# Second feed-forward product of a hybrid encoder layer: four accumulators a row pair, last chunk in two groups of rows, first operands made during the first product

## The chip, the cores and the metric

One core of one Trainium2 chip. The metric is the device time of one execution in microseconds (us); three executions are shown for the kernel before, and one further execution was recorded by the hardware profiler. All durations below are of that profiled execution.

## The reference, cut to what matters

The input is 2048 rows of 1024 numbers, in float32. One layer mixes them (a gated MLP and a gated linear attention), projects, and adds; this part takes about the first 780 us and its arithmetic is not touched. Then comes the feed-forward part:

```
f = rmsnorm(h, pre_ff_g) @ w_ff1          # 2048 x 1024 times 1024 x 4096
f = square(relu(f)) @ w_ff2               # 2048 x 4096 times 4096 x 1024
h = h + rmsnorm(f, post_ff_g)             # the output
```

The change concerns the second of these products, its normalisation, and the passage from the first product to the second.

## The kernel before, in words

**Numbers in two parts.** Every matmul operand is a pair: `hi`, rounded to a shorter format by the scalar engine (ACT), and `lo`, the rest, a subtraction on the vector engine (DVE). One product of two such operands is three matmuls (`mm3`, lines 142 to 145): high by low, high by high, low by high, each 128x128 by 128x512.

**Seven products in place of eight.** Both feed-forward products go by a Strassen-Winograd scheme (`WINO`, lines 40 and 41): of two 2x2 blocked operands seven block products p1 to p7 are made, from sums s1 to s4 of the left blocks and t1 to t4 of the right ones. p1, p6, p7 and p4 are added up in one PSUM bank (chain A), p5 and p3 in a second one (C), p2 in a third (B). Read after each step, the banks hold what the output blocks need: block 11 is p1 plus p2, block 12 is A after p6 plus C after p3, block 22 is A after p7 plus C after p5, block 21 is A after p4.

**The first product** (lines 696 to 927) runs in 224 ticks of 12 matmuls: 2 halves of the rows (p) by 16 pieces of the 4096 columns (q) by 7 products. Its results go to memory (`f_d`, written by `keep_f`, lines 859 to 866). The sums and splits of `w_ff2` are also made during it and stored as 1 MB tiles (`t_d`, lines 823 to 829). DVE, ACT, GpSimd (POOL) and SyncE (SP) follow an order written out by hand (`plan`, `do`, `tick`); line 928 closes that order.

**The second product** (lines 934 to 1133) has 16 chunks, 0 to 15: 2 halves of the rows (p) by 8 pieces of the 4096 terms (c). A chunk has 28 slots: 7 products (order `SECOND`, line 46) by 4 row blocks r; a slot is 6 matmuls (2 pieces kk by `mm3`). For each product the right operand is a 1 MB tile `tt`, read by `read_t` (lines 981 to 985) two products ahead into one of three buffers. The left operands come from `f_d`: `read_f` (lines 943 to 948, 512 KB each, four a chunk, into the four `xr` tiles), `sum_f`, `high_f` (ACT) and `low_f` (DVE). Before the loop all operands of chunk 0 are made (lines 1017 to 1030) in an order that the framework chooses; from line 1032 on the order is again that of the program. There `PREP` (lines 988 to 995) says in which slot of the chunk before each of the 22 steps of a chunk comes (two casts and two sums first, the last step in slot 23), `SHIFT` by how many slots later, `READ` that the next chunk's tiles are read in the slots 18 to 21 of this count.

**Out of PSUM** (`evac`, lines 1065 to 1091): after each slot its bank is added to an accumulator. There are seven a row pair, one for each product and r, 28 tiles (line 1069). In the first piece (c = 0) ACT copies, afterwards DVE adds; in the last piece DVE also folds three of the seven into others (lines 1076 to 1079), and the four that remain are the blocks 11, 12, 21, 22.

**The end of a row.** `square_sum` (ACT) sums the squares of each finished half row; `root` (two DVE operations of one column and a power on POOL, line 153) makes the factor; `scale` (DVE, line 1059) multiplies; `give` (line 1062) adds the row of h that `read_h` brought, and sends the half row out (256 KB). For the first half of the rows these steps wait in the list `tail` and are worked off from chunk 8 on, one or two a slot, and `give` is on DVE, its transfer on POOL's queue. For the second half they follow two slots after the last product; there `give` is on POOL for the rows of block 21 and 22 and on DVE for the others.

**Where tiles lie.** Pools are stacked from the left and from the right end of SBUF. During the first product the right side holds `wq` (the split pieces of `w_ff1`) and `fr` (20 tiles of the right operand and 3 staging tiles `w2s`), the left one `big`. When they close, `g` takes the place of `big` on the left, and `ga` (accumulators) and then `gt` (the three `tt` buffers) that of `wq` and `fr`. A tile in the new place waits for the last use of what lay there.

## Time and profile before

| | us |
|---|---|
| three executions | 2084.5, 2089.95, 2090.33 (median 2089.95) |
| the profiled execution | 2087.72 |
| its span, first to last instruction | 2085.9 |
| DVE busy | 1424.2 (68%) |
| ACT busy | 995.7 (48%) |
| POOL busy | 253.4 (12%) |
| mean granted TensorE clock | 0.989 of full |
| moved by DMA | 446.85 MB, 214 GB/s on the mean |

The profiled execution is 2.2 us below the median and 1.8 us longer than its span. The first feed-forward product begins shortly before 790 us of the span, the second at about 1426. Busy times are sums over stages with different limits; what a stage is worth is read from the stage's own rows. In the timeline a row gives the start, the time, the engine and line, the operation with output and inputs, and in brackets how long the engine was idle before it and what ended that.

### The profile page before, as it was taken

How to read it: one execution, taken by the hardware profiler on the slowest of the kernel's cores; microseconds unless marked ns; L12 is line 12 of the kernel's file. 1: busy time of each engine (PE TensorE's matmuls, PEld its weight loads, DVE VectorE, ACT ScalarE, POOL GpSimd, SP SyncE). 2: the span in 40 equal slices, each digit the busy share in tenths (PEclk: the TensorE clock that was granted, in tenths of full speed). 3: DMA queues.
4: the chain of work that ended last, by engine and by line, in shares of the span. 5: the costliest groups of instructions: out<-in, count | busy, mean ns of one | idle time of the engine just before them, and what ended most of it. 6: DMA issues, size and time to landing. Idle time of an engine off the chain costs nothing.

```text
span 2085.9 us, 27424 instructions
## 1 busy us (share of the span) xinstructions
PE 2014.2 (97%) x9504; PEld 1656.1 (79%) x9504; DVE 1424.2 (68%) x2483; ACT 995.7 (48%) x1966; POOL 253.4 (12%) x407
## 2 busy tenths in 40 slices
PE   8999999999899998999998999997999999999995
PEld 6889887888788877888887788886888888788884
DVE  4484457357736676656668666765688888889887
ACT  5463465346444565556667666665412215312212
POOL 0020011001101200013321333320000001100003
PEclk9999999999999999999999999999999999999998
DMA  7444244425842546858879888776666767876754
GB/s 214 124 117 128 81 142 143 152 72 165 266 162 87 176 167 204 268 181 271 281 254 307 282 277 284 270 254 246 249 255 234 262 242 261 344 274 231 268 196 181
DMA packets 164715, 446.85 MB, mean 214 GB/s; under 512 B 23376, under 2 KB 48480, under 8 KB 150240
## 3 DMA queue, kind: packets, MB, share of 16 engines
q1 hardware_dynamic: 139040, 359.09, 50.9%
q0 software_dynamic: 25536, 86.00, 11.4%
q8 instruction: 75, 1.23, 0.2%
q14 instruction: 64, 0.52, 0.1%
HBM read 319.19 MB, written 125.83 MB: 213 GB/s over the span
## 4 chain that ended last, share of the span: by engine, by line
PE 76%; DMA 9%; DVE 5%; issue 4%; ACT 3%; POOL 2%; SPq 0%; POOLq 0%; DVEq 0%; ACTq 0%
PE po_A L143 5%; PE po_A L144 5%; PE po_A L145 5%; PE pf_A L143 5%; PE pf_A L144 4%; PE pf_A L145 4%; PE pp_o L143 3%; PE po_C L143 3%; PE pp_o L145 2%; PE po_C L144 2%; PE po_C L145 2%; PE pp_o L144 2%; PE pf_C L145 2%; PE pf_C L144 2%; PE pf_C L143 2%
## 5 line engine op out<-in xcount | busy, mean ns | idle before, releaser
L493 DVE TENSOR_TENSOR acc_p<-acc_p,po_A 128x512 f32<-128x512 f32 x224 | 154.1, 688 | 34.9 <-PE po_A L145 20.5
L974 ACT CAST sh_s<-r 128x512 fp32r<-128x512 f32 x96 | 56.6, 619 | 187.0 <-PE po_A L145 109.5
L140 DVE TENSOR_TENSOR wl_s<-s,wh_s 128x512 fp32r<-128x512 f32 x96 | 66.2, 690 | 67.3 <-ACT wh_s L691 67.2
L143 PE MATMUL pf_A<-hl_t,wh_s 128*128 128x512 f32 x256 | 101.8, 398 | 9.5 <-ACT uy L894 6.1
L143 PE MATMUL po_A<-tt,sh_s 128*128 128x512 f32 x256 | 101.0, 394 | 6.1 <-ACT acc_p L1070 2.4
L143 PE MATMUL pp_o<-wl_o,abh 128*128 128x512 f32 x256 | 103.4, 404 | 2.2 <-DVE h L450 2.0
L143 PE MATMUL po_C<-tt,sh_s 128*128 128x512 f32 x256 | 101.3, 396 | 3.0 <-DMA tt<-t_d_t 3.0
L144 PE MATMUL pf_A<-hh_t,wh_s 128*128 128x512 f32 x256 | 101.5, 396 | 0.0
L145 PE MATMUL pf_A<-hh_t,wl_s 128*128 128x512 f32 x256 | 101.2, 395 | 0.0
L218 DVE SCALAR_TENSOR_TENSOR wl_o<-ws_o,outg,wh_o 128x512 fp32r<-128x512 f32 x64 | 47.9, 750 | 78.0 <-ACT wh_o L217 78.0
L144 PE MATMUL po_C<-tt,sh_s 128*128 128x512 f32 x256 | 100.8, 394 | 0.0
L974 ACT CAST sh_a<-f 128x512 fp32r<-128x512 f32 x94 | 55.8, 619 | 94.2 <-DMA f<-f_d 46.0
L145 PE MATMUL po_C<-tt,sl_s 128*128 128x512 f32 x256 | 100.5, 393 | 0.0
L145 PE MATMUL pp_o<-wh_o,abl 128*128 128x512 f32 x256 | 100.5, 393 | 0.0
L144 PE MATMUL po_A<-tt,sh_s 128*128 128x512 f32 x256 | 100.2, 391 | 0.0
L144 PE MATMUL pp_o<-wh_o,abh 128*128 128x512 f32 x256 | 100.1, 391 | 0.0
L145 PE MATMUL po_A<-tt,sl_s 128*128 128x512 f32 x256 | 99.8, 390 | 0.0
L143 PE MATMUL po_A<-tt,sh_a 128*128 128x512 f32 x248 | 97.4, 393 | 0.0
L144 PE MATMUL po_A<-tt,sh_a 128*128 128x512 f32 x248 | 97.1, 391 | 0.0
L145 PE MATMUL po_A<-tt,sl_a 128*128 128x512 f32 x248 | 96.6, 390 | 0.0
L140 DVE TENSOR_TENSOR wl_a<-w1s,wh_a 128x512 fp32r<-128x512 f32 x96 | 65.9, 687 | 43.4 <-ACT wh_a L691 43.4
L217 ACT ACTIVATE wh_o<-ws_o,outg 128x512 fp32r<-128x512 f32 x64 | 46.3, 723 | 100.6 <-PE pp_o L145 56.2
(298 smaller groups left out, 6043.6 us busy)
## 6 DMA issues: line engine op xcount, KB each, us to landing
tt<-t_d_t SPq DMA_DIRECT2D x64, 1024.0 KB, 4.9
tt<-t_d_b SPq DMA_DIRECT2D x48, 1024.0 KB, 4.8
w1s<-in_w SPq DMA_DIRECT2D x64, 512.0 KB, 4.8
f<-f_d SPq DMA_DIRECT2D x64, 512.0 KB, 7.0
ws_o<-in_w_out SPq DMA_DIRECT2D x64, 256.0 KB, 2.5
w2s<-in_w POOLq DMA_DIRECT2D x32, 512.0 KB, 6.2
t_d_t<-th_t POOLq DMA_DIRECT2D x64, 256.0 KB, 4.8
t_d_t<-tl_t POOLq DMA_DIRECT2D x64, 256.0 KB, 4.6
```

The lines of the kernel that those rows point to most:

```text
L140: v.tensor_tensor(out_lo, src, hi.bitcast(F32), ALU.subtract)
L143: pe.matmul(ps, ahi, blo, start=start, stop=False, **kw)
L144: pe.matmul(ps, ahi, bhi, start=False, stop=False, **kw)
L145: pe.matmul(ps, alo, bhi, start=False, stop=stop, **kw)
L217: a.activation(hi, st, AF.Copy, scale=gain)
L218: v.scalar_tensor_tensor(lo, st, gain, hi.bitcast(F32), ALU.mult, ALU.subtract)
L493: eng.tensor_tensor(out_, x_, y_, ALU.add)
L974: a.copy(hi, src)
```

## The change

- Four accumulators a row pair (11, 12, 22, 21) instead of seven, and 24 tiles for them instead of 28. In the first piece ACT copies the products p1, p6, p5 and p4 into them and DVE adds p7, p3 and p2; after that DVE adds all seven. Nothing is folded in the last piece.
- The last chunk runs in two groups of rows: all seven products for r = 0 and 1, then all seven for r = 2 and 3. Its seven `tt` tiles stay until the second group has used them: three in `gt`, two in the four `xr` tiles (in halves), one in `w2s` tiles (halves), one in four accumulator tiles (quarters).
- `some` works the list `tail` off by one step a slot in the last chunk, and in three of four slots of chunk 7 and each slot of chunk 8. All `give` additions are on DVE. The rows of h for the last chunk are asked for on POOL's queue, all within the slots 2 and 3 of that chunk.
- The left operands of chunk 0 are begun during the last 14 ticks of the first product: four `read_f`, the first `tt` (into `w2s` tiles), the two splits of a11 and the two sums s1. The rest of chunk 0 stands in the slots from -4 on: `SHIFT` is 20 for chunk 0, 16 for chunk 1, then 14, 12, 10, 8, 6, 5, and 4 for chunk 8.
- The pool `wq` moves to the left side; the staging tiles `w2s` become a pool of their own, `br`, that is not closed; `gt` is laid before `ga`. The hand-written order of DVE, ACT, POOL and SP isn't closed between the products. The last `keep_f` and the gain `pfg` go over POOL's queue.

`read_f`, `sum_f`, `high_f` and `low_f` move up unchanged.

```diff
+NACC = 24
...
-    wq = wqp.enter_context(tc.tile_pool(name="wq", bufs=1, side="right", reuse_waits="tile"))
+    wq = wqp.enter_context(tc.tile_pool(name="wq", bufs=1, reuse_waits="tile"))
...
-        nonlocal fr
+        nonlocal fr, br
         if hf == 0 and k == 1:
             mixp.close()
+            br = ctx.enter_context(tc.tile_pool(name="br", bufs=1, side="right", reuse_waits="tile"))
             fr = frp.enter_context(tc.tile_pool(name="fr", bufs=1, side="right", reuse_waits="tile"))
...
-    first = ctx.enter_context(ExitStack())
-    first.enter_context(tc.manual_schedule(engines={ENG.DVE, ENG.Activation, ENG.Pool, ENG.SP}))
+    ctx.enter_context(tc.manual_schedule(engines={ENG.DVE, ENG.Activation, ENG.Pool, ENG.SP}))
...
-        xr = fr.tile([P, D], F32, name=f"xq{i}", tag="w2s", bufs=3)
+        xr = br.tile([P, D], F32, name=f"xq{i}", tag="w2s", bufs=3)
...
-            dma.dma_start(f_d[p][q][:, n, :], us[s][4][n])
+            (dma if s + 1 < NST else pool).dma_start(f_d[p][q][:, n, :], us[s][4][n])
...
+    def read_t(j):
+
+
+        src = t_d[chunks[j // 7][1]][WINO[SECOND[j % 7]][1]]
+        where = {0: "br", 7 * NCH - 7: "xr", 7 * NCH - 6: "xr", 7 * NCH - 5: "br", 7 * NCH - 4: "acc"}.get(j, "tt")
+        if where == "tt":
+            tt = gt.tile([P, 2, 2, 512], F32R, name=f"tt{j}", tag="tt", bufs=3)
+            dma.dma_start(tt.bitcast(F32), src)
+            tts[j] = [[tt[:, kk, m, :] for m in range(2)] for kk in range(2)]
+        elif where == "acc":
+            tts[j] = [[ga.tile([P, 512], F32R, name=f"tt{j}_{kk}_{m}", tag="acc", bufs=NACC) for m in range(2)]
+                      for kk in range(2)]
+            for kk in range(2):
+                for m in range(2):
+                    dma.dma_start(tts[j][kk][m].bitcast(F32), src[:, kk, m, :])
+        else:
+            pool_, tag, bufs = (br, "w2s", 3) if where == "br" else (wp, "xr", 4)
+            two = [pool_.tile([P, 2, 512], F32R, name=f"tt{j}_{kk}", tag=tag, bufs=bufs) for kk in range(2)]
+            for kk in range(2):
+                dma.dma_start(two[kk].bitcast(F32), src[:, kk])
+            tts[j] = [[t[:, m, :] for m in range(2)] for t in two]
+
+
+    end = len(seq)
+    for t, fn, *args in (
+        (end - 14, read_f, 0, 0, 0), (end - 11, read_f, 0, 0, 1), (end - 8, read_t, 0), (end - 7, read_f, 0, 1, 0),
+        (end - 4, read_f, 0, 1, 1), (end - 4, high_f, 0, "a11", 0), (end - 4, low_f, 0, "a11", 0),
+        (end - 3, sum_f, 0, "s1", 0), (end - 2, high_f, 0, "a11", 1), (end - 2, low_f, 0, "a11", 1),
+        (end - 1, sum_f, 0, "s1", 1),
+    ):
+        plan(t, fn, *args)
...
-    first.close()
     frp.close()
     bigp.close()
     wqp.close()
 
 
     g = ctx.enter_context(tc.tile_pool(name="g", bufs=1, reuse_waits="tile"))
+    gt = ctx.enter_context(tc.tile_pool(name="gt", bufs=1, side="right", reuse_waits="tile"))
     ga = ctx.enter_context(tc.tile_pool(name="ga", bufs=1, side="right", reuse_waits="tile"))
-    gt = ctx.enter_context(tc.tile_pool(name="gt", bufs=1, side="right", reuse_waits="tile"))
     pfg = wp.tile([P, D], F32, name="pfg", tag="pg")
-    dma.dma_start(pfg, post_ff_g.partition_broadcast(P))
...
+    pool.dma_start(pfg, post_ff_g.partition_broadcast(P))
...
-        key = WINO[SECOND[j % 7]][1]
-        tts[j] = gt.tile([P, 2, 2, 512], F32R, name=f"tt{j}", tag="tt", bufs=3)
-        dma.dma_start(tts[j].bitcast(F32), t_d[chunks[j // 7][1]][key])
...
-    SHIFT = {NC: 12, NC + 1: 12, NC + 2: 9, NC + 3: 6, NC + 4: 3}
+    SHIFT = {0: 20, 1: 16, 2: 14, 3: 12, 4: 10, 5: 8, 6: 6, 7: 5, NC: 4, NC + 1: 12, NC + 2: 9, NC + 3: 6, NC + 4: 3}
...
-    for m in range(1, NCH):
+    for m in range(NCH):
         o = 28 * (m - 1) + SHIFT.get(m, 0)
         for n, what, name, kk in PREP:
+            if m == 0 and n < 4:
+                continue
             if what == "sum":
                 plan2(o + n, sum_f, m, name, kk)
             else:
 
-                plan2((o + n, 0), high_f, m, name, kk)
+                plan2(o + n - 0.5, high_f, m, name, kk)
                 plan2(o + n, low_f, m, name, kk)
         if m + 1 < NCH:
             for n, half, kk in READ:
                 plan2(o + n, read_f, m + 1, half, kk)
 
-    for n in range(2):
-        for kk in range(2):
-            read_f(0, n, kk)
-    read_t(0)
     read_t(1)
-    for n, what, name, kk in PREP:
-        if what == "sum":
-            sum_f(0, name, kk)
-        else:
-            high_f(0, name, kk)
-            low_f(0, name, kk)
-    for n in range(2):
-        for kk in range(2):
-            read_f(1, n, kk)
-
-    ctx.enter_context(tc.manual_schedule(engines={ENG.DVE, ENG.Activation, ENG.Pool, ENG.SP}))
+    for t in sorted(t for t in todo2 if t < -0.5):
+        for fn, args in todo2.pop(t):
+            fn(*args)
+
     halves, res = {}, {}
...
-                dma.dma_start(res[i][hf], h_d[i][:, hf * 512:(hf + 1) * 512])
+                pool.dma_start(res[i][hf], h_d[i][:, hf * 512:(hf + 1) * 512])
...
-    def give(i, hf, eng, queue):
-        plus(eng, res[i][hf], res[i][hf], halves[i, hf])
+    def give(i, hf, queue):
+        plus(v, res[i][hf], res[i][hf], halves[i, hf])
         queue.dma_start(out[i * P:(i + 1) * P, hf * 512:(hf + 1) * 512], res[i][hf])
+
+
+    INTO = {"p1": 11, "p2": 11, "p6": 12, "p3": 12, "p5": 22, "p7": 22, "p4": 21}
 
     def evac(m, n, r, ps_):
         p, c = chunks[m]
-        x_ = acc.get((p, n, r))
-        if c == 0:
-            acc[p, n, r] = ga.tile([P, 512], F32, name=f"acc{p}_{n}_{r}", tag="acc", bufs=28)
-            a.copy(acc[p, n, r], ps_)
-            return
-        plus(v, x_, x_, ps_)
-        if c < NC - 1:
+        key = p, INTO[n], r
+        if c == 0 and n in ("p1", "p6", "p5", "p4"):
+            acc[key] = ga.tile([P, 512], F32, name=f"acc{p}_{INTO[n]}_{r}", tag="acc", bufs=NACC)
+            a.copy(acc[key], ps_)
+        else:
+            plus(v, acc[key], acc[key], ps_)
+        if c < NC - 1 or n not in ("p7", "p4", "p3", "p2"):
             return
         i, j = p * 2 * NPAIR + r, p * 2 * NPAIR + NPAIR + r
-        if n in ("p1", "p6", "p5"):
-            y_ = acc[p, {"p1": "p2", "p6": "p3", "p5": "p7"}[n], r]
-            plus(v, y_, y_, x_)
-            return
         row_, hf = {"p7": (j, 1), "p4": (j, 0), "p3": (i, 1), "p2": (i, 0)}[n]
-        halves[row_, hf] = x_
+        halves[row_, hf] = acc[key]
         square_sum(row_, hf)
         if hf:
             return
         soon.setdefault(slot_ + 1, []).append((root, row_))
-        if p < NP - 1:
-            tail.extend(((scale, row_, 1), (give, row_, 1, v, pool), (scale, row_, 0), (give, row_, 0, v, pool)))
-        else:
-            eng = pool if row_ == j else v
-            soon.setdefault(slot_ + 2, []).extend((
-                (scale, row_, 1), (give, row_, 1, eng, dma), (scale, row_, 0), (give, row_, 0, eng, dma)))
+        queue = pool if p < NP - 1 else dma
+        for h_ in (1, 0):
+            tail.append((slot_ + 2, scale, row_, h_))
+            tail.append((slot_ + 2, give, row_, h_, queue))
+        if p < NP - 1 and row_ == j:
+
+            tail.append((slot_ + 2, read_h, i - 2) if r > 1 else (0, int))
+        if p < NP - 1 and row_ == i and r < 2:
+            tail.append((slot_ + 2, read_h, i + 2))
+
+    def some(heavy):
+
+        while tail and tail[0][0] <= slot_ and heavy > 0:
+            _, fn, *args = tail.pop(0)
+            fn(*args)
+            heavy -= fn is not read_h
 
     slot_ = 0
     for m, (p, c) in enumerate(chunks):
         banks = {}
-        for n7, n in enumerate(SECOND):
-            name, key, chain = WINO[n]
-            j = 7 * m + n7
-            if j + 2 < 7 * NCH:
-                read_t(j + 2)
-            tt = tts.pop(j)
-            for r in range(NPAIR):
-                begun = (chain, r) in banks
-                if not begun:
-                    banks[chain, r] = bank(f"po{m}_{chain}_{r}", "mm" if chain == "A" else "mx")
-                rs = slice(r * P, (r + 1) * P)
-                for kk in range(2):
-                    hi, lo = left[m, name, kk]
-                    mm3(banks[chain, r], hi[:, rs], lo[:, rs], tt[:, kk, 0, :], tt[:, kk, 1, :],
-                        kk == 0 and not begun, kk == 1, skip_group_check=True)
-                for fn, args in todo2.pop((slot_, 0), ()):
-                    fn(*args)
-                evac(m, n, r, banks[chain, r])
-                for fn, args in todo2.pop(slot_, ()):
-                    fn(*args)
-                for fn, *args in soon.pop(slot_, ()):
-                    fn(*args)
-                for _ in range((2 if slot_ % 4 == 3 else 1) if c < NC - 1 else 0):
-                    if tail:
-                        fn, *args = tail.pop(0)
+        final = m == NCH - 1
+        for grp in ((0, 1), (2, 3)) if final else (range(NPAIR),):
+            for n7, n in enumerate(SECOND):
+                name, key, chain = WINO[n]
+                j = 7 * m + n7
+                if grp[0] == 0 and j + 2 < 7 * NCH:
+                    read_t(j + 2)
+                for r in grp:
+                    begun = (chain, r) in banks
+                    if not begun:
+                        banks[chain, r] = bank(f"po{m}_{chain}_{r}", "mm" if chain == "A" else "mx")
+                    rs = slice(r * P, (r + 1) * P)
+                    for kk in range(2):
+                        hi, lo = left[m, name, kk]
+                        mm3(banks[chain, r], hi[:, rs], lo[:, rs], *tts[j][kk], kk == 0 and not begun, kk == 1,
+                            skip_group_check=True)
+                    for fn, args in todo2.pop(slot_ - 0.5, ()):
                         fn(*args)
-
-                        nth = 8 - len(tail) // 4
-                        if len(tail) % 4 == 0 and 2 <= nth < 6:
-                            read_h(nth - 2)
-                if c == NC - 1 and n7 == 3:
-                    read_h(p * 2 * NPAIR + NPAIR + r)
-                if c == NC - 1 and n7 == 4 and p == NP - 1:
-                    read_h(p * 2 * NPAIR + r, True)
-                slot_ += 1
+                    evac(m, n, r, banks[chain, r])
+                    for fn, args in todo2.pop(slot_, ()):
+                        fn(*args)
+                    for fn, *args in soon.pop(slot_, ()):
+                        fn(*args)
+                    some(1 if c == 0 or c == NC - 1 and (final or slot_ % 2) or slot_ % 4 == 0 else 0)
+                    if c == NC - 1 and n7 == 1:
+                        rows = [NPAIR + r] if not final else [NPAIR + r, r, NPAIR + r + 2, r + 2][:4]
+                        if grp[0] == 0:
+                            for row_ in rows:
+                                read_h(p * 2 * NPAIR + row_, final and row_ % NPAIR > 1)
+                    slot_ += 1
     for t in sorted(soon):
         for fn, *args in soon[t]:
             fn(*args)
+    for _, fn, *args in tail:
+        fn(*args)
 
 
 def _constants():
```

## Rows read from the trace of the kernel before

**Rows 1.** The page, section 1: busy time, share of the span, instructions.
```profile
PE 2014.2 (97%) x9504; PEld 1656.1 (79%) x9504; DVE 1424.2 (68%) x2483; ACT 995.7 (48%) x1966; POOL 253.4 (12%) x407
```
**Rows 2.** Stretches: length, busy us (instructions) of PE, PEld, DVE, ACT, POOL; clock, DMA, GB/s.
```profile
1426.50:1479.40 52.90, 42.53 (x170) 33.64 (x170) 23.81 (x37) 29.06 (x53) 2.18 (x4) 0.94 0.82 311
1479.40:1518.00 38.60, 38.60 (x171) 31.66 (x170) 31.87 (x50) 9.93 (x17) 0.00 (x0) 1.00 0.67 246
1748.80:1787.20 38.40, 38.40 (x170) 31.50 (x169) 30.73 (x53) 21.66 (x41) 11.34 (x20) 1.00 0.95 363
...
2060.50:2085.90 25.40, 7.18 (x18) 4.85 (x18) 17.45 (x33) 4.72 (x14) 6.38 (x8) 0.60 0.33 124
```
**Rows 3.** Timeline of PE, from the first product to chunk 1 of the second.
```profile
1426.13 0.40 PE L145 MATMUL pf_C<-hh_b,wl_s 128*128 128x512 f32 x1
...
1431.41 0.79 PE L143 MATMUL po_A<-tt,s_a 128*128 128x512 f32 x1 [4.88 <-DMA tt<-t_d_b]
...
1450.11 0.51 PE L143 MATMUL po_C<-tt,sh_s 128*128 128x512 f32 x1 [3.05 <-DMA tt<-t_d_t]
...
1479.30 0.39 PE L143 MATMUL po_A<-tt,sh_a 128*128 128x512 f32 x1
```
**Rows 4.** Timeline of PE, its two waits at the start of chunk 9.
```profile
1794.37 0.50 PE L143 MATMUL po_A<-tt,sh_s 128*128 128x512 f32 x1 [1.78 <-DVE acc_p L493]
...
1807.54 0.47 PE L143 MATMUL po_A<-tt,sh_s 128*128 128x512 f32 x1 [1.91 <-DMA tt<-t_d_t]
```
**Rows 5.** Timeline of PE, chunk 15: its first matmul, its longest wait, its last matmul.
```profile
2021.87 0.39 PE L143 MATMUL po_A<-tt,sh_a 128*128 128x512 f32 x1
...
2060.85 0.50 PE L143 MATMUL po_B<-tt,sh_a 128*128 128x512 f32 x1 [2.66 <-DVE acc_p L493]
...
2068.68 0.60 PE L145 MATMUL po_B<-tt,sl_a 128*128 128x512 f32 x1
```
**Rows 6.** DMA issues (KB each, median us to landing), and the landings of tile f.
```profile
tt<-t_d_t SPq DMA_DIRECT2D x64, 1024.0 KB, 4.9
...
f<-f_d SPq DMA_DIRECT2D x64, 512.0 KB, 7.0
...
hr<-h_d POOLq DMA_DIRECT2D x12, 512.0 KB, 8.3
...
DMA to landing us min/median/max: 3.5/7.0/12.3
```
**Rows 7.** Timelines of ACT and DVE around the first product's end.
```profile
1415.59 1.14 ACT L974 CAST s_a<-f 128x512 fp32r<-128x512 f32 x2
...
1426.57 0.69 DVE L493 TENSOR_TENSOR uy<-uy,pf_C 128x512 f32<-128x512 f32 x1 [5.24 <-PE pf_C L145]
1427.17 1.29 DVE L140 TENSOR_TENSOR sl_s<-r,sh_s 128x512 fp32r<-128x512 f32 x2
...
1427.29 0.63 ACT L856 ACTIVATE uy<-uy 128x512 f32<-128x512 f32 x1 [1.23 <-DVE uy L493]
```
**Rows 8.** Timeline of PE, two waits early in the first product.
```profile
797.93 0.50 PE L143 MATMUL pf_A<-hl_t,wh_s 128*128 128x512 f32 x1 [3.20 <-ACT u L894]
...
812.23 0.50 PE L143 MATMUL pf_C<-hl_b,wh_s 128*128 128x512 f32 x1 [1.79 <-DVE hl_b L140]
```
**Rows 9.** Timelines of POOL and DVE in the last 37 us.
```profile
2049.59 2.99 POOL L493 TENSOR_TENSOR hr<-hr,acc_p 128x512 f32<-128x512 f32 x2 [1.21 <-DVE acc_p L1059]
...
2050.09 1.26 DVE L1053 TENSOR_TENSOR ssf<-ssf 128x1 f32<-128x1 f32 x1
...
2078.35 0.15 DVE L152 TENSOR_SCALAR rs_f<-ssf 128x1 f32<-128x1 f32 x1
2079.23 0.75 DVE L1059 SCALAR_TENSOR_TENSOR acc_p<-acc_p,rs_f,pfg 128x512 f32<-128x512 f32 x1 [0.73 <-POOL rs_f L153]
2080.02 0.69 DVE L493 TENSOR_TENSOR hr<-hr,acc_p 128x512 f32<-128x512 f32 x1
...
2081.41 0.69 DVE L493 TENSOR_TENSOR hr<-hr,acc_p 128x512 f32<-128x512 f32 x1
```

More of the change, by code (lines that the diff above doesn't have):

```diff
@@ L755, in ht_in @@
             if n % 2 == 0:
-                staged["two"] = fr.tile([P, D], F32, name=f"hr{p}_{n}", tag="w2s", bufs=3)
+                staged["two"] = br.tile([P, D], F32, name=f"hr{p}_{n}", tag="w2s", bufs=3)
             st = staged["two"][:, n % 2 * H:(n % 2 + 1) * H]
@@ L776, in sums_in @@
         for c in range(2):
-            st = fr.tile([P, D], F32, name=f"hs1_{k}_{c}", tag="w2s", bufs=3)
+            st = br.tile([P, D], F32, name=f"hs1_{k}_{c}", tag="w2s", bufs=3)
             for n in range(2):
@@ L810, in read_w2 @@
         i = 2 * q + n
-        st = fr.tile([P, D], F32, name=f"w2s{q}_{n}", tag="w2s", bufs=3)
+        st = br.tile([P, D], F32, name=f"w2s{q}_{n}", tag="w2s", bufs=3)
         pool.dma_start(st, w2[i * P:(i + 1) * P, :])
@@ L912, in tick @@
             plan(i + 1, keep_f, s, 1)
-    for n in range(2):
-        read_w1(0, n)
-    for t in range(3):
-        read_x(t)
-    for n in range(2):
-        read_w1(1, n)
-    for i in sorted(j for j in todo if j < 0):
-        do(i)
-    norm_m()
-    residual(0)
-    for i in range(len(seq)):
-        tick(i)
-    for i in sorted(todo):
-        do(i)
-    first.close()
-    frp.close()
-    bigp.close()
-    wqp.close()
-    g = ctx.enter_context(tc.tile_pool(name="g", bufs=1, reuse_waits="tile"))
-    ga = ctx.enter_context(tc.tile_pool(name="ga", bufs=1, side="right", reuse_waits="tile"))
-    gt = ctx.enter_context(tc.tile_pool(name="gt", bufs=1, side="right", reuse_waits="tile"))
-    pfg = wp.tile([P, D], F32, name="pfg", tag="pg")
-    dma.dma_start(pfg, post_ff_g.partition_broadcast(P))
     chunks = [(p, c) for p in range(NP) for c in range(NC)]
@@ new lines, in trunk @@
+    end = len(seq)
[6 more added lines that the diff above has]
+        plan(t, fn, *args)
+    for n in range(2):
+        read_w1(0, n)
+    for t in range(3):
+        read_x(t)
@@ new lines, in trunk @@
+    for n in range(2):
+        read_w1(1, n)
+    for i in sorted(j for j in todo if j < 0):
+        do(i)
+    norm_m()
+    residual(0)
+    for i in range(len(seq)):
+        tick(i)
+    for i in sorted(todo):
+        do(i)
+    frp.close()
+    bigp.close()
+    wqp.close()
+    g = ctx.enter_context(tc.tile_pool(name="g", bufs=1, reuse_waits="tile"))
+    gt = ctx.enter_context(tc.tile_pool(name="gt", bufs=1, side="right", reuse_waits="tile"))
+    ga = ctx.enter_context(tc.tile_pool(name="ga", bufs=1, side="right", reuse_waits="tile"))
@@ L988, in trunk @@
+    pfg = wp.tile([P, D], F32, name="pfg", tag="pg")
+    pool.dma_start(pfg, post_ff_g.partition_broadcast(P))
     PREP = (
```

4 lines of the change are left out of this document (1 added, 3 removed).

## The prediction, made before the changed kernel ran

> **What bounds the kernel now.** I read the page first: TensorE is busy 97% of the span [rows 1], so only its idle stretches and the time after its last matmul can be won. Then the busy time by stretches [rows 2]: a chunk without trouble (1479.4 to 1518.0) has PE busy throughout at full clock, chunk 0 (1426.5 to 1479.4) has the same number of matmuls in 52.9 us, with the clock at 0.94 and the DMA share at 0.82, and the last 25 us have 18 matmuls. PE's timeline gives the places. Chunk 0 begins 4.9 us after the first product's last matmul, waiting for its `tt`, waits 3.05 us more for the `tt` of p5, and ends at 1479.30 [rows 3]. At the start of chunk 9 there are two short waits, 1.78 us for DVE and 1.91 us for a `tt` [rows 4]. In the last chunk, which begins at 2021.87, p2 waits for DVE (the longest time 2.66 us), and the last matmul starts at 2068.68 [rows 5]. From chunk 1's start to chunk 15's are 2021.87 - 1479.30 = 542.6 us; less the two waits that is 538.9 over 14 chunks, **38.5 us a chunk, 1.375 us a slot**. Against that, chunk 0 loses 1479.3 - 1426.4 - 38.5 = **14.4 us**, the start of chunk 9 3.7, and, as chunk 15 at this pace would be done at 2060.5, **25.4 us** of the span lie behind the earliest possible end of the matmuls.
>
> **Part 1: first operands during the first product.** L is the end of the first product's last matmul. p1 of chunk 0 needs its `tt` and the splits of a11. The `tt` is asked for 8 ticks before the end; a tick of 12 matmuls is 2.75 us, so 22 us ahead of a transfer that takes 4.9 [rows 6]. The f tiles are asked for 14, 11, 7 and 4 ticks ahead and used 10, 9, 4 and 3 ticks later, 8.2 us in the tightest case against a median landing of 7.0 [rows 6]; the worst of 12.3 would hold DVE about 4 us, but in the very last tick, where nothing but chunk 0 is behind it. So p1 should begin at L. p6 follows four slots later, at L + 5.5, and needs the splits of s2, which are placed behind L. DVE starts its last addition of the first product 0.05 us after L and then goes at 0.6 us an operation ([rows 7]: two in 1.29): that addition, the second s1, two sums s2, by L + 2.5. ACT has two operations for the last result (0.63 each [rows 7]), then the two casts, done by about L + 3.3; DVE's two `lo` by L + 4.1. That is 1.4 us early. The second `tt` (p6) lies in `gt`, now on the place of right-operand tiles last used by p7, two ticks before the end; asked for at L - 5.5 it is there at L. Copies of p1 out of PSUM lie between ACT's casts, the first at about L + 4.5, also ahead of p6. I price what is left at 1.0 us (nothing at the least; at the most the 4.9 + 3.05 us of today's two `tt` waits [rows 3]). Saved: 13.4.
>
> The extra work in the first product's last 14 ticks (four casts and subtractions, two sums) is what DVE and ACT do there today as well (two casts of a11 stand 11 us ahead of L [rows 7]). Three transfers go to POOL's queue, which has no other work at L. The moved pools `wq` and `br` change only which dead tiles a new one waits for, at the first product's start: 0, bounds -2 to +3 by the waits of 1.79 and 3.20 us that PE has there [rows 8].
>
> **Part 2: four accumulators.** DVE's additions: 12 fold operations fewer in each last piece, 12 more in each first piece, where ACT did 28 copies and now does 16. No operation is saved in all; it is moved. In chunk 15 that takes 12 x 0.6 = 7.2 us off DVE, in chunks 0 and 8 it adds as much. Chunk 0 bears it: 12 additions and some 30 steps are 25 us of 38.5. Chunk 8 has `tail` too. In the last ten slots of chunk 7 DVE has 10 additions, 8 steps for chunk 8, 6 of `tail` (0.7 each: a `scale` and `give` pair is 1.4 us, 2080.02 to 2081.41 [rows 9]) and 6 roots of 0.35: 17.1 us in 13.7, **3.4 us behind**. It catches up in the first 12 slots of chunk 8, where it has only `tail`. In the slots 12 to 26 it has 15 steps, 15 of `tail` and 11 additions: 9 + 10.5 + 6.6 = 26.1 us in 20.6, so **5.5 us behind** when chunk 9 begins. p6 of chunk 9 needs p1's bank emptied within three slots, 4.1 us; the addition itself takes 0.7, so DVE may be 3.4 late, and PE waits 2.1 us. The rows of h are asked for about five slots (6.9 us) ahead of their use, against 8.3 us [rows 6] under a DMA share of 0.95 [rows 2]: 1.4 more, once, as a DVE that is late covers the next. So 3.5 in place of 3.7 (bounds 0 and 7): saved 0.2.
>
> **Part 3: the last chunk in two groups.** Group 1 is done after 14 slots; its 16 steps of `tail` fill the slots 10 to 25, one beside one addition, 0.6 + 0.7 = 1.3 of 1.375 us. The slots 26 and 27 take two of group 2's 16. A bank now has one slot between two uses, not three: 1.375 us less the addition's 0.75 leaves 0.6, and roots (0.35) use it up in places; I take 0.5 us of PE waits. After the last matmul's end: the last addition (0.7), its squares on ACT (0.8), the root: L' + 1.95. Then 14 steps, 7 pairs of 1.4 = 9.8, to L' + 11.75; from the end of the last `give` at 2082.1 to the span's end are 3.8 us [rows 9, 2]. Together 15.5 in place of 25.4: saved 9.9 - 0.5 = 9.4. No `give` is on POOL now. Today two of them take 2.99 us there and beside them a DVE addition of one column takes 1.26 us, where the root's other operation takes 0.15 [rows 9]; that cost goes and is contained in the 25.4.
>
> The last chunk's `tt` tiles are needed twice as fast. From the freeing of `xr` tiles in slot 17 of chunk 14 to p2's first slot (12 of chunk 15) are 23 slots, 31.6 us, and in it fall eight `tt` and six rows of h: 8 x 1.05 + 6 x 0.52 = 11.5 MB, 365 GB/s. The trace shows 363 GB/s at a DMA share of 0.95 for 38 us [rows 2], so it just fits; the rows of h, asked for from slot 24 on and needed 20 us later, are behind most of the `tt`. I take 0; the upper bound is that all 3.1 MB go ahead, 8.7 us. [...]
>
> **The sum.** 2087.7 - 13.4 - 0.2 - 9.4 = **2064.7 us**, taken against the profiled execution, which is 2.2 below the median and within the spread of the three runs (2084.5 to 2090.3). I forecast 2065.
>
> **The rivals.**
> 1. *The first operands do not come in time* (the change does not do what it says). `tt` for p6 waits for something that lives until L, as today's first one does, and goes out with the gain, the last f and 2 MB of h. For it: today's three come late in just this crowd. Against: it lies on other tiles, and four f reads are gone from the crowd. Price: up to 4.9 + 3.05 and the slow clock behind them, some 7 us: 2072.
> 2. *The last chunk starves.* The rows of h go ahead of `tt` tiles on a second queue. For it: 365 GB/s wanted, 363 seen. Against: most `tt` are asked for 8 slots ahead. Price up to 8.7, say 7: 2072.
> 3. *Slower: late f tiles hold DVE in every chunk.* `SHIFT` leaves 6 slots between reading and first use in chunk 1 and 8 or 9 in chunks 2 to 8, where 10 were (8 slots: 11 us). DVE would wait in its fixed order and PE for it from a landing of 11 + 3.4 = 14.4 us on; at 19 us it would be 4.6 x 8 = 37 us: 2065 + 37 = 2102. It decides from about 18 us on. Against it: the worst landing today is 12.3 [rows 6], and by the old `SHIFT` the chunks 10 to 13 had only 7 slots, and PE did not wait there.
>
> **How the numbers follow.** A difference under 0.3% (6 us) can hardly be told from none here. Forecast (2058 to 2069): 0.66. Rival 1: 0.17, rival 2: 0.10. Rival 3: 0.03. Rivals 1 and 2 together with a bad chunk 9 and pools that wait, within 6 us of today: 0.04. The lower end is 2065 less 1.0, 3.5, 0.5 and about 2.5 of spread; the upper takes in rivals 1 and 2 with the median's 2.2: 2057.5 to 2075. Faster 0.93, same 0.04, slower 0.03.
>
> **What would show it.** Right: chunk 0 of 38.5 to 40 us at full clock, no PE wait of over 1 us at the change of products; one or two waits of 1 to 4 us for DVE early in chunk 9; in the last chunk no wait over 0.5 us, and about 15.5 us from the last matmul to the end, filled with pairs of `scale` and `give`. Wrong: PE waiting for `tt` in chunk 0 (rival 1) or 15 (rival 2), for DVE behind an f read in chunks 1 to 8 (rival 3); or a tail over 18 us.

## The result and the profile after

| | before | after |
|---|---|---|
| executions, us | 2084.5 to 2094.65 (5), median 2089.95 | 2055.21 to 2059.88 (5), median 2057.36 |
| the profiled execution | 2087.72 | 2057.67 |
| its span | 2085.9 | 2055.7 |

The ratio is 0.9848, 95% interval 0.9827 to 0.9869: 1.5% faster. 2057.36 lies 0.1 us under the lower end of the range given (2057.5 to 2075) and 7.6 us below the forecast of 2065. Cut at the starts of PE's rows, the two profiled spans compare like this (the last column is what the prediction took off):

| stretch | before | after | difference | forecast |
|---|---|---|---|---|
| to the first matmul of the first product | 781.8 | 781.6 | -0.2 | 0 |
| the first product, first to last matmul | 644.4 | 638.1 | **-6.3** | 0 |
| from there to the end of chunk 0 | 53.2 | 38.8 | -14.4 | -13.4 |
| chunks 1 to 14 | 542.6 | 541.9 | -0.7 | -0.2 |
| chunk 15 and what is behind it | 64.1 | 55.4 | -8.7 | -9.4 |
| together | 2085.9 | 2055.7 | -30.2 | -23.0 |

The three parts of the forecast came within 1.0 us each. What it had not seen is the second line.

The timeline of PE in the changed kernel, the last matmuls of the first product, the first of chunk 0 and of chunk 1 (start, time, engine and line, operation, idle time before it; compare [rows 3]):

```profile
1419.71 0.39 PE L146 MATMUL pf_C<-hh_b,wl_s 128*128 128x512 f32 x1
1419.94 0.40 PE L144 MATMUL po_A<-tt,s_a 128*128 128x512 f32 x1
...
1458.49 0.39 PE L144 MATMUL po_A<-tt,sh_a 128*128 128x512 f32 x1
```

The second product's first matmul starts 0.23 us behind the first product's last one, as any next matmul does. The busy times of the changed kernel by stretches: chunks 0, 1, 8, 9, 15, and what follows the last matmul (length, then busy us and instructions of PE, PEld, DVE, ACT, POOL, granted clock, DMA share, GB/s; compare [rows 2]):

```profile
1419.94:1458.49 38.55, 38.55 (x169) 31.55 (x168) 27.00 (x42) 20.05 (x36) 3.21 (x6) 1.00 0.79 290
1458.49:1496.95 38.46, 38.46 (x170) 31.55 (x168) 33.70 (x53) 9.61 (x18) 0.00 (x0) 1.00 0.68 246
1727.67:1766.62 38.95, 38.81 (x170) 31.32 (x168) 32.23 (x58) 16.82 (x35) 12.21 (x20) 1.00 0.98 373
1766.62:1808.08 41.46, 38.98 (x169) 31.39 (x168) 38.49 (x62) 10.83 (x20) 2.17 (x4) 1.00 0.75 275
2000.35:2040.98 40.63, 39.61 (x169) 31.12 (x167) 30.69 (x57) 10.65 (x29) 6.76 (x10) 1.00 0.55 218
2040.98:2055.70 14.72, 0.00 (x0) 0.00 (x0) 11.32 (x21) 0.93 (x4) 1.77 (x2) 0.63 0.40 151
```

Chunk 0 now takes what chunk 1 takes, at full clock. The last matmul is followed by 14.7 us. PE's waits that are left in the second product are two in chunk 9 (compare [rows 4]) and three in chunk 15 (compare [rows 5]):

```profile
1773.65 0.50 PE L144 MATMUL po_A<-tt,sh_s 128*128 128x512 f32 x1 [1.37 <-DVE acc L494]
...
1786.02 0.47 PE L144 MATMUL po_A<-tt,sh_s 128*128 128x512 f32 x1 [1.10 <-DMA tt<-t_d_t]
...
2012.13 0.47 PE L144 MATMUL po_A<-tt,sh_a 128*128 128x512 f32 x1 [0.53 <-DMA tt<-t_d_t]
...
2015.47 0.47 PE L144 MATMUL po_C<-tt,sh_s 128*128 128x512 f32 x1 [0.33 <-DMA tt<-t_d_b]
...
2018.63 0.50 PE L144 MATMUL po_B<-tt,sh_a 128*128 128x512 f32 x1 [0.15 <-DMA tt<-t_d_b]
```

And DVE's timeline: the last addition of chunk 8, then the first `scale` and the last `give` behind the last matmul (compare [rows 9]):

```profile
1771.71 0.68 DVE L494 TENSOR_TENSOR acc<-acc,po_B 128x512 f32<-128x512 f32 x1
...
2042.81 0.74 DVE L1076 SCALAR_TENSOR_TENSOR acc<-acc,rs_f,pfg 128x512 f32<-128x512 f32 x1
...
2051.91 0.69 DVE L494 TENSOR_TENSOR hr<-hr,acc 128x512 f32<-128x512 f32 x1
```

**Where the 6.3 us of the first product are.** They are not in its waits: PE waits some seven times in it, 12.1 us in all before and 13.6 after. In stretches without a wait PE is never idle and the clock is 1.00 in both kernels, but the matmuls follow each other faster. Nine matmuls of p2 at its end, before (1391.95 - 1389.85 = 2.10 us, 233 ns each) and after (1385.91 - 1383.87 = 2.04, 227 ns each):

```profile
1389.85 0.39 PE L145 MATMUL pf_B<-hh_b,wl_a 128*128 128x512 f32 x1
...
1391.95 0.39 PE L145 MATMUL pf_B<-hh_b,wl_a 128*128 128x512 f32 x1
```
```profile
1383.87 0.39 PE L146 MATMUL pf_B<-hh_b,wl_a 128*128 128x512 f32 x1
...
1385.91 0.39 PE L146 MATMUL pf_B<-hh_b,wl_a 128*128 128x512 f32 x1
```

Over all 2688 matmuls the paces fall into few values, and they change exactly where the right operand's tiles lie in another pool: before, tiles of `big` (p1, p2, p4, p3 and half of p6) go at 233.3 ns and those of `fr` at 226.8 (p5 and p7; the other half of p6, right behind `big`, at 230); after, most of `big` at 226.7 and `fr` at 229.5. With the matmuls right behind each change of pool the means are 233.3 and 227.6 before, 227.6 and 229.5 after: 1728 x 5.7 - 960 x 1.9 = 8.0 us less, of which the longer waits, with the slower matmuls right behind them (behind three of the seven waits of each kernel six to eight of them stand 0.42 to 0.43 us apart), take 1.7 back. By the addresses that the build gives the tiles, left and right don't start at the same place: modulo 256 bytes of a partition the tiles of `big`, on the left, begin at 160, those of `wq` and `fr`, on the right, at 224. A matmul's stationary tile is in `wq`, its moving one in `big` or `fr`; the change takes `wq` from the right to the left, where its tiles begin at 160. So the **theory** (A): the pace goes by the distance of the moving from the stationary tile, modulo some 2^n bytes. The **rivals**: it goes by the side (B), or the gain comes from something else in the change (C).

### The profile page after: what moved, and what is told of

The parts are those of the page before. It is cut to its first block, busy times and chain, and to the rows that moved or that the text cites. A ratio compares the mean times of both kernels' runs of the same rounds, so it can differ in the third digit from the quotient of the medians.

```text
span 2055.7 us, 27515 instructions
## 1 busy us (share of the span) xinstructions
PE 1999.5 (97%) x9504; PEld 1654.6 (80%) x9504; DVE 1422.9 (69%) x2491; ACT 979.5 (48%) x1942; POOL 250.7 (12%) x410
## 4 chain that ended last, share of the span: by engine, by line
PE 75%; DMA 9%; DVE 6%; issue 4%; ACT 3%; POOL 2%; SPq 0%; POOLq 0%; DVEq 0%; ACTq 0%
PE po_A L144 5%; PE po_A L145 5%; PE po_A L146 5%; PE pf_A L144 5%; PE pf_A L146 5%; PE pf_A L145 4%; PE pp_o L144 3%; PE pp_o L146 3%; PE pp_o L145 3%; PE po_C L144 2%; PE po_C L145 2%; PE po_C L146 2%; PE pf_C L144 2%; PE pf_C L146 2%; PE pf_C L145 2%
## 5 line engine op out<-in xcount | busy, mean ns | idle before, releaser
L494 DVE TENSOR_TENSOR acc<-acc,po_A 128x512 f32<-128x512 f32 x232 | 159.3, 687 | 47.3 <-PE po_A L146 33.0
L950 ACT CAST sh_s<-r 128x512 fp32r<-128x512 f32 x96 | 55.6, 618 | 165.4 <-PE po_A L146 92.9
L144 PE MATMUL pf_A<-hl_t,wh_s 128*128 128x512 f32 x256 | 102.5, 400 | 10.6 <-ACT uy L895 6.9
L494 DVE TENSOR_TENSOR acc<-acc,po_C 128x512 f32<-128x512 f32 x120 | 82.5, 687 | 21.4 <-PE po_C L146 14.0
```

What stands on the lines that cost most here:

```text
L144: pe.matmul(ps, ahi, blo, start=start, stop=False, **kw)
L494: eng.tensor_tensor(out_, x_, y_, ALU.add)
L950: a.copy(hi, src)
```

## The experiments

Each is one edit of the kernel before or after. The table has the stretches of the profiled execution of each, cut as above ("each of 1 to 7" is one of these chunks):

| kernel | median, us | ratio to before, interval | first product | to the end of chunk 0 | each of 1 to 7 | 8 and 9 | 15 to the end |
|---|---|---|---|---|---|---|---|
| before | 2087 to 2090 | | 644.4 | 53.2 | 38.45 | 81.1 | 64.1 |
| after | 2057.4 | 0.9848, 0.9827 to 0.9869 | 638.1 | 38.8 | 38.45 | 80.4 | 55.4 |
| wq_left | 2082.7 | 0.9963, 0.9951 to 0.9974 | 637.1 | 53.6 | 38.45 | 81.8 | 63.8 |
| before_gap | 2074.6 | 0.9923, 0.9900 to 0.9945 | 631.1 | 49.6 | 38.08 | 82.6 | 63.8 |
| after_gap | 2051.4 | 0.9818, 0.9793 to 0.9842 | 634.7 | 38.5 | 38.08 | 81.5 | 55.8 |
| after_skew192 | 2067.8 | 0.9899, 0.9875 to 0.9923 | 645.5 | 38.8 | 38.45 | 82.0 | 56.1 |
| after_skew64 | 2068.8, one execution | | 639.7 | 38.8 | 38.45 | 79.5 | 55.6 |
| after_skew256 | 2060.4, one execution | | 639.1 | 38.8 | 38.45 | 79.5 | 55.7 |
| late_first | 2064.6 | 0.9890, 0.9871 to 0.9909 | 638.6 | 43.4 | 38.45 | 81.3 | 55.6 |
| one_group | 2063.5 | 0.9884, 0.9864 to 0.9904 | 638.1 | 38.8 | 38.45 | 80.4 | 59.4 |
| four_acc | 2091.2 | 1.0011, 0.9994 to 1.0027 | 644.2 | 54.1 | 38.45 | 84.1 | 64.1 |
| gives_dve | 2089.5 | 1.0007, 0.9993 to 1.0022 | 644.9 | 51.4 | 38.45 | 82.6 | 63.6 |
| gap_tail | 2052.0 | 0.9832, 0.9811 to 0.9854 | 632.3 | 38.5 | 38.08 | 82.5 | 55.9 |
| gap_spread | 2047.6 | 0.9806, 0.9782 to 0.9830 | 633.9 | 38.5 | 38.08 | 79.3 | 56.6 |

What comes ahead of the first product varies (781 to 787 us, and 791.9 in after_skew64), and so does the old chunk 0 in kernels that leave it as it was (49.6 to 54.1); chunks 8 and 9 vary in kernels that don't touch them too (81.1 to 82.6 like before, 79.5 to 82.0 like after), and the first product of the three changed kernels with a gap by 2.4 us, in its waits and the slower matmuls behind them; the other stretches repeat to some tenths. A difference of 1 or 2 us in chunks 8 and 9 is therefore not shown by one profile.

### Where the tiles lie

**wq_left**, the kernel before with that one line of the change:

```diff
-    wq = wqp.enter_context(tc.tile_pool(name="wq", bufs=1, side="right", reuse_waits="tile"))
+    wq = wqp.enter_context(tc.tile_pool(name="wq", bufs=1, reuse_waits="tile"))
```

> The kernel before, with the one edit that the weight pool wq lies on the left of SBUF, as in the changed kernel. Theory A (the pace of a matmul depends on how far apart, modulo 512 bytes, its moving and its stationary tile start): the first product's 1728 matmuls whose moving tile is in big go from 233.3 to about 227.6 ns, the 960 with a tile of fr from 227.7 to 229.5; 1728 x 5.7 - 960 x 1.8 = 8 us, so 2082 in place of 2090. Theory B (it depends on whether both lie on the same side of SBUF): the same 8 us here. Theory C (the first product's 6 us come from br, from the moved steps or from the queues): no change, within 2 us.

It gave 2082.7, and the first product 637.1, 7.3 us less than before. C falls: this line alone accounts for the 6.3 us. A and B both stand.

**before_gap**, the kernel before, and **after_gap**, the changed one, with 320 bytes left free:

```diff
     wqp = ctx.enter_context(ExitStack())
+    gap = ctx.enter_context(tc.tile_pool(name="gap", bufs=1, side="right"))
+    gap.tile([P, 80], F32, name="gap")
```

To make room, after_gap, gap_tail and gap_spread also keep 8 in place of 9 of the small `rs` buffers of the second product (not in the cut above).

> The kernel before, all pools where they were, and 320 unused bytes a partition at the right end of SBUF, so that every tile of the right side starts 320 bytes lower and left and right tiles start at the same place modulo 512. Theory A: all of the first product at 226.7 ns (5.0 x 2688 = 13.4 us less) and the second at 226.7 in place of 228.9 (5.9 us less): about 19 us, 2071. Theory B: nothing changes, as no tile changes its side: 2090. Theory C: 2090.

> The changed kernel with the same 320 bytes at the right end (and one small buffer of 32 bytes fewer, to make room). Theory A: first product from a mean of 228.8 to 226.7 ns (2.1 x 2688 = 5.6 us less), second from 228.9 to 226.7 (5.9 us less; a chunk takes 38.1 in place of 38.45), so about 2046. Theory B: 2057.

**after_skew192**, **after_skew64** and **after_skew256**, the changed kernel with 192, 64 and 256 bytes left free between the stationary and the moving tiles of the first product (n = 48, 16, 64):

```diff
+    gap = bigp.enter_context(tc.tile_pool(name="gap", bufs=1))
+    gap.tile([P, n], F32, name="gap")
     big = bigp.enter_context(tc.tile_pool(name="big", bufs=1, reuse_waits="tile"))
```

> The changed kernel with 192 unused bytes between wq and big, both on the left: moving tile less stationary tile is then 192 modulo 512, as in the kernel before. Theory A: the 1728 matmuls of the first product whose moving tile is in big go back to 233.3 ns, 1728 x 5.7 = 10 us more, 2067; the second product as it was. Theory B: both stay on the left, so 2057.

> The changed kernel with 64 unused bytes between wq and big: in the first product the moving tiles of big start 64 bytes behind the stationary ones, modulo 512. Theory A1 (the pace goes by the distance modulo 256, of which 320 is 64): these 1728 matmuls take about 229 ns, as those at 320 do; the first product 3 to 4 us longer. Theory A2 (it goes by the distance modulo 512, and 64 is near 0): 226.7 as in the changed kernel.

> The changed kernel with 256 unused bytes between wq and big. Theory A1 (modulo 256): the same 226.7 ns as at distance 0, the time unchanged. Theory A2 (modulo 512): another pace, between the 233.3 measured at 192 and the 229 at 320, so 4 to 10 us more in the first product.

The same two stretches of 200 us of each kernel, in the first and in the second product (columns as above; to read is the count of PE's matmuls, at full clock and without idle time). Before:

```profile
1200.00:1400.00 200.00, 200.00 (x868) 162.08 (x867) 139.28 (x224) 131.70 (x235) 62.55 (x116) 1.00 0.80 275
1500.00:1700.00 200.00, 200.00 (x876) 164.09 (x875) 169.78 (x263) 43.98 (x74) 0.00 (x0) 1.00 0.68 245
```

After:

```profile
1200.00:1400.00 200.00, 200.00 (x878) 164.47 (x877) 140.46 (x225) 132.64 (x236) 61.47 (x114) 1.00 0.82 280
1500.00:1700.00 200.00, 200.00 (x876) 164.09 (x875) 172.20 (x266) 40.72 (x72) 0.00 (x0) 1.00 0.70 255
```

before_gap:

```profile
1200.00:1400.00 200.00, 200.00 (x884) 165.68 (x883) 141.39 (x226) 134.83 (x241) 59.43 (x110) 1.00 0.81 278
1500.00:1700.00 200.00, 200.00 (x884) 165.58 (x884) 169.67 (x261) 40.88 (x69) 0.00 (x0) 1.00 0.70 248
```

after_gap:

```profile
1200.00:1400.00 200.00, 200.00 (x884) 165.62 (x883) 140.52 (x225) 134.46 (x240) 59.48 (x110) 1.00 0.84 283
1500.00:1700.00 200.00, 200.00 (x884) 165.62 (x883) 174.01 (x269) 42.51 (x75) 0.00 (x0) 1.00 0.71 257
```

after_skew192:

```profile
1200.00:1400.00 200.00, 200.00 (x865) 162.29 (x864) 139.47 (x224) 132.59 (x236) 62.26 (x116) 1.00 0.80 274
```

after_skew64:

```profile
1200.00:1400.00 200.00, 200.00 (x876) 164.10 (x875) 141.18 (x228) 134.62 (x240) 62.21 (x116) 1.00 0.82 280
```

868 matmuls before, 878 after, 884 in both kernels where left and right are brought to the same place, and 865 where `big` was pushed back by 192 bytes, though nothing changed its side: B falls. The gap moves the second product too, 876 to 884, 38.08 us a chunk in place of 38.45, as A had it. By groups of matmuls, from start to start:

| moving less stationary, modulo 256 | which | ns |
|---|---|---|
| 0 | `fr` before (p5, p7); p4 after and in after_skew256; all of the two kernels with the gap | 226.7 to 227.3 |
| 64 | `fr` after; `big` in after_skew64; the second product, before and after | 228.9 to 229.5 |
| 160 | chunk 0's p1 in after_gap (23 matmuls) | 234.0 |
| 192 | `big` before and in after_skew192 | 233.1 to 233.3 |
| 224 | chunk 0's p1 without the gap; in the changed kernels chunk 15's p1 and p6, whose `tt` lie in `xr` | 232.9 to 233.5 |

64 and 256 bytes came out by A1: 64 goes like the 320 of `fr`, 256 like 0. That the pace goes by the distance modulo 256 rests on these two pairs; both are single executions, so they are read by the pace, not by the time. That it is the distance, and not the place of one of the two tiles, is seen at 0 and 192, which each came with two pairs of places: 0 with both tiles at 224 (before) and both at 160 (after), 192 with moving and stationary at 160 and 224 (before) and at 96 and 160 (after_skew192). The medians gained less than A's sums for the two gaps, 15 and 6 us in place of 19 and 11 (the profiled execution of before_gap, the fastest of its four, gained 18). The paces came as expected, but some waits of PE grew: chunks 8 and 9 of after_gap take 5.3 us more than two clean ones, 3.5 in the changed kernel. That the engines beside PE have less time a slot would explain it; it was not tried.

The count of matmuls in these rows differs by 2% (868 before, 884 in before_gap) at full clock with nothing but the place changed. Which part of the chip makes it so, no run shows.

### The parts of the change

**late_first**, the changed kernel without the steps planned into the first product:

```diff
-    end = len(seq)
-    for t, fn, *args in (
-        (end - 14, read_f, 0, 0, 0), (end - 11, read_f, 0, 0, 1), (end - 8, read_t, 0), (end - 7, read_f, 0, 1, 0),
...
-        plan(t, fn, *args)
...
+    for n in range(2):
+        for kk in range(2):
+            read_f(0, n, kk)
+    read_t(0)
     read_t(1)
+    for kk in range(2):
+        high_f(0, "a11", kk)
+        low_f(0, "a11", kk)
+    for kk in range(2):
+        sum_f(0, "s1", kk)
```

> The changed kernel without the steps planned into the first product: chunk 0's f tiles, its first tt, the splits of a11 and the sums s1 are asked for and made behind the first product's last matmul. Theory A (part 1 is worth about the 13.4 us forecast, because these steps are early): PE waits some 8 us for f (landing 7.0), cast and subtraction, and some 5 us more for tt and for s2 under the slow clock; about 2070. Theory B (most of the 14 us came from the places of the tt tiles, which no longer wait for a tile that lives until the end of the first product): only the f chain of 8 us comes back, 2065.

2064.6: 7.3 us more than the changed kernel, the time that B gave, though not by the chain that B named, so in part by luck. PE waits once, for a cast, and of the matmuls behind it six follow each other 0.42 to 0.43 us apart, where from 1428.06 us on it is 0.23 again (the mean granted clock is 0.63 in the second row; columns as above):

```profile
1423.91 0.50 PE L144 MATMUL po_A<-tt,s_a 128*128 128x512 f32 x1 [2.61 <-ACT s_a L950]
```
```profile
1423.91:1428.50 4.59, 4.59 (x12) 3.37 (x13) 4.51 (x8) 1.95 (x4) 0.81 (x2) 0.63 1.00 417
```

The f tiles were there: SP issued the four reads, which stand behind the first product in the program, from 1406.5 us on, 14 us before the first product's last matmul. No `tt` is waited for. So of the 14.4 us the early steps are 4.6 (53.2 and 38.8 against 43.4; the rest of the 7.3 lies in stretches that the edit doesn't touch and in the spread of the medians). The other 9.8, or 6 to 11 by the spread of the old chunk 0, come from the rest of the change. In it the new places of the `tt` tiles are the likely cause, as both of the old waits [rows 3] were for a `tt` and both are gone here; they were not tried alone.

**one_group**, the changed kernel with the last chunk in one group:

```diff
-        for grp in ((0, 1), (2, 3)) if final else (range(NPAIR),):
+        for grp in (range(NPAIR),):
...
-                        if grp[0] == 0:
+                        if not final or r < 2:
```

> The changed kernel with the last chunk's four rows in one group, as in the other chunks; four accumulators and all gives on DVE stay. Theory A (the two groups carry the 9.4 us of part 3): about 2066. Theory B (half of them came from the twelve additions and the POOL gives that go with the rest of the change): of 32 steps 12 are done by the end of the matmuls, 20 x 0.7 + 1.95 + 3.1 = 19 us behind the last one in place of 14.7, with no waits for tt any more, so 2060 to 2062.

2063.5, between the two. Its chunk 15 has no wait (38.85 us), and 20.5 follow the last matmul, columns as above:

```profile
1999.96:2038.81 38.85, 38.84 (x169) 31.37 (x167) 25.41 (x49) 10.62 (x29) 6.07 (x10) 1.00 0.50 198
2038.81:2059.30 20.49, 0.00 (x0) 0.00 (x0) 16.95 (x29) 0.96 (x4) 2.51 (x3) 0.57 0.42 161
```

Two groups take 5.8 us off the end (20.5 to 14.7) and cost 1.8 in the chunk (40.63 to 38.85): 4.0 of part 3's 8.7. The other 4.7 are there without them: up to the start of its last matmul the chunk takes 38.4 us in place of 46.8, with no wait and the clock at 1.00, and 3.7 of that is lost again behind it.

**four_acc**, the kernel before with the four accumulators alone:

```diff
+    INTO = {"p1": 11, "p2": 11, "p6": 12, "p3": 12, "p5": 22, "p7": 22, "p4": 21}
...
-        x_ = acc.get((p, n, r))
-        if c == 0:
+        key = p, INTO[n], r
+        if c == 0 and n in ("p1", "p6", "p5", "p4"):
...
-        if n in ("p1", "p6", "p5"):
-            y_ = acc[p, {"p1": "p2", "p6": "p3", "p5": "p7"}[n], r]
-            plus(v, y_, y_, x_)
-            return
```

> The kernel before with four accumulators a row pair in place of seven and nothing else. Theory A (the twelve additions less in the last chunk let p2 go on): PE's waits for DVE in chunk 15, 5.5 us in all, go, chunk 9 keeps its two waits; 2084 to 2086. Theory B (as the forecast has it, part 2 is worth 0.2 by itself): 2089 to 2090, as DVE's 7.2 us in chunk 15 turn up in chunks 8 and 9.

No difference, as B had it. p2's waits in the last chunk stay, without the twelve additions:

```profile
2065.13 0.50 PE L143 MATMUL po_B<-tt,sh_a 128*128 128x512 f32 x1 [1.54 <-DVE acc L493]
...
2069.43 0.51 PE L143 MATMUL po_B<-tt,sh_a 128*128 128x512 f32 x1 [2.65 <-DVE acc L493]
...
2072.41 0.79 PE L143 MATMUL po_B<-tt,sh_a 128*128 128x512 f32 x1 [0.78 <-DVE acc L493]
```

Chunks 8 and 9 take 3.0 us more than before, 1.5 to 3.0 more than in the kernels that leave them as they were (81.1 to 82.6): alone, the four accumulators seem to cost there part of what DVE has to do in addition. With the rest of the change (79.5 to 82.0) no cost is seen.

**gives_dve**, the kernel before with all gives on DVE:

```diff
-            eng = pool if row_ == j else v
+            eng = v
```

> The kernel before with one edit: in the last chunk's gives of rows j the addition is made by DVE in place of POOL. Theory A (p2's three waits for DVE and the slow clock behind them, 8.4 us of chunk 15, come from POOL: its gives of 2.95 us hold the roots, and DVE's one-column additions of 1.26 us stand beside them): DVE is through a row j in 3.75 us in place of 4.33 though it does two gives more, so 2 to 3 us less waiting and 2086 to 2088. Theory B (they come from the four steps of a row that stand in one place ahead of p3's additions, whoever does the gives): 2090 or a little more.

Also no difference. A's 2 to 3 us less waiting did not come: the three waits are 5.5 us in all, as before. To the last matmul's start chunk 15 does take 44.6 us in place of 46.8, because the granted clock is 1.00 in it and not 0.93, but what follows is 1.7 us longer, as DVE has more to do there (12.4 us in place of 10.6). The three waits, and chunk 15 of the kernel before and of this one (columns as above):

```profile
2056.32 0.50 PE L143 MATMUL po_B<-tt,sh_a 128*128 128x512 f32 x1 [1.39 <-DVE acc_p L493]
...
2060.16 0.50 PE L143 MATMUL po_B<-tt,sh_a 128*128 128x512 f32 x1 [2.19 <-DVE acc_p L493]
...
2063.75 0.51 PE L143 MATMUL po_B<-tt,sh_a 128*128 128x512 f32 x1 [1.93 <-DVE acc_p L493]
```
```profile
2021.87:2068.68 46.81, 41.35 (x168) 32.75 (x167) 37.66 (x60) 10.52 (x30) 14.46 (x13) 0.93 0.55 202
```
```profile
2021.81:2066.40 44.59, 39.09 (x169) 31.13 (x167) 38.35 (x66) 9.81 (x28) 2.32 (x5) 1.00 0.58 212
```

So neither the additions nor POOL's gives hold the old last chunk by themselves, as far as intervals of 0.15% (3 us) can tell. For the 4.7 us the likeliest that is left is that a row's four steps no longer stand in one place but one a slot; that was not tried alone.

### A faster kernel

**gap_tail** and **gap_spread**, after_gap with the steps of `tail` sooner or later:

```diff
-                    some(1 if c == 0 or c == NC - 1 and (final or slot_ % 2) or slot_ % 4 == 0 else 0)
+                    some(2 if c == 0 and slot_ % 28 < 4 else 1 if c == 0 or c == NC - 1 and (final or slot_ % 2) or slot_ % 4 == 0 else 0)
```
```diff
-                    some(1 if c == 0 or c == NC - 1 and (final or slot_ % 2) or slot_ % 4 == 0 else 0)
+                    some(1 if c == 0 and (slot_ % 28 < 8 or slot_ % 3 == 0) or c == NC - 1 and (final or slot_ % 2) or slot_ % 4 == 0 else 0)
```

> The changed kernel with the 320 bytes of after_gap, and in chunk 8's first four slots two steps of tail a slot in place of one, as DVE stands idle there for 5.1 us before p6's first result. Theory A (PE's waits in chunks 8 and 9, 5.3 us over two clean chunks of 38.08, are DVE's delay and nothing else): 3 to 5 us less than after_gap, 2047 to 2048. Theory B (the steps then wait for their rows of h, and what is behind them with them): as after_gap, 2051 to 2053.

> after_gap with the steps of tail slower in place of faster: from slot 8 of chunk 8 on one in three slots, the rest in chunk 9. Theory A (DVE is behind because chunk 8's own steps and tail's fall together in its second half, and what gap_tail ran into was the rows of h, of which only four have a place): PE's waits in chunks 8 and 9 go from 5.3 to 1 us or less, 2047. Theory B (tail's steps in chunk 9 then hold DVE there): 2051 to 2053.

gap_tail came out by B. In after_gap DVE idles 5.10 us before p6's first result in chunk 8:

```profile
1739.63 0.69 DVE L496 TENSOR_TENSOR acc<-acc,po_A 128x512 f32<-128x512 f32 x1 [5.10 <-PE po_A L148]
```

In gap_tail the time was no use to it; it stands 6.97 us for a row of h, whose tile is free only when an earlier row has gone out:

```profile
1743.43 0.69 DVE L496 TENSOR_TENSOR hr<-hr,acc 128x512 f32<-128x512 f32 x1 [6.97 <-DMA out<-hr]
```

gap_spread went half of A's way: chunks 8 and 9 take 3.2 us over two clean ones in place of 5.3 (columns as above), not 1, and one wait for DVE moved to p4 of chunk 9. These chunks vary as much in kernels that leave them alone, so it is not shown that the slower steps did it:

```profile
1721.97:1761.23 39.26, 38.65 (x169) 31.38 (x168) 30.15 (x56) 19.17 (x39) 10.04 (x16) 1.00 0.92 338
1761.23:1801.30 40.07, 38.61 (x169) 31.38 (x168) 37.30 (x62) 8.52 (x16) 2.70 (x5) 1.00 0.74 276
```

At 2047.6 it has the lowest median; against after_gap (2051.4) the intervals overlap, and the profiled spans are alike (2048.3 and 2048.4). That the two kernels with a gap are faster than the changed one is shown by their stretches: 3.4 to 4.2 us less in the first product, 0.37 in each clean chunk.

## Why the prediction was right, and where not

The three parts named gave 23.8 us where 23.0 were forecast. The 7.6 us by which the time lies under the forecast, and just under the range, are the first product's 6.3 and small differences; the forecast had that term at 0.

- **Part 1** (13.4 us): 14.4. Chunk 0 is clean, and even the 1.0 left for small waits wasn't needed. The reason given covers both halves, the early steps and the `tt` that no longer waits for a tile which lives until L; the prediction put its weight on the steps, which are 4.6 of it: the size was right, the reason in part. Rival 1 didn't come: no `tt` is late in chunk 0.
- **Part 2** (0.2): 0.7, a difference within the spread of chunks 8 and 9. DVE was said to be 5.5 us behind when chunk 9 begins at 1766.6; its last addition of chunk 8 starts at 1771.7, 4.7 behind the matmuls' end at about 1767.0. PE waits 1.4 for it, not 2.1, and 1.1 for a `tt`, as was feared.
- **Part 3** (9.4): 8.7. The end came as summed: 7 pairs of `scale` and `give` from 2042.8 to 2052.6 are 9.8, and 14.7 us in place of 15.5, because the last transfer takes 3.1 and not 3.8. PE waits 1.0 us in three places, not 0.5 for DVE but for `tt`: rival 2 in small. The sum was made of the new end as a whole and holds as such. As for the reasons, the groups are 4.0 of it; the additions and the gives, named beside them, gave nothing by themselves, and where the other 4.7 come from stays open.
- **The DMA bound.** The prediction took 363 GB/s for about the most that the trace shows and let 8.7 us stand as the bound. The trace of before has more, 424 over 11 us of chunk 0 and 389 over 38 us of chunks 8 and 9:

```profile
1441.00:1452.00 11.00, 6.39 (x26) 4.82 (x26) 5.36 (x8) 5.79 (x11) 0.00 (x0) 0.97 1.02 424
1759.00:1797.00 38.00, 36.22 (x159) 29.41 (x158) 30.16 (x48) 19.70 (x36) 11.26 (x21) 1.00 0.99 389
```

  In the changed kernel 11 us of the last chunk moved 413:

```profile
2003.00:2014.00 11.00, 10.47 (x46) 8.26 (x45) 5.01 (x8) 1.45 (x4) 0.55 (x1) 1.00 1.03 413
```

  These rows, 413 and 424 at a DMA share of 1.02 to 1.03, are 14 and 17% above the 363, so that figure is not the most that this core moves; where the bound lies, no run shows.
- **The step that failed** is the last sentence of part 1: "The moved pools `wq` and `br` change only which dead tiles a new one waits for [...]: 0, bounds -2 to +3." They change the pace of the first product's matmuls, 6.3 us, outside both bounds. The rows to see it were in the trace of before: the bounds were taken from the waits early in the first product [rows 8], and the starts of matmuls that wait for nothing were left aside. They stand 233 ns apart with tiles of one pool and 227 with those of another.
- **Rival 3** didn't come: chunks 1 to 7 take 38.45 us each, as before.
